# Linear attention in a one-layer encoder kernel: block exponentials with a bias column instead of differences, the root's square on ScalarE, the norm weight in the gate rows, and two filler banks with four for small products

## The chip, the cores and the metric

The kernel runs on one core of a Trainium2 chip. The metric is the device time of one execution in microseconds (us). The kernel before took 1954.07 us (median of three runs, 1953.86 to 1955.78).

## The reference

One layer for 1056 frames at once: a prompt of 1024 and a sample of 32 that goes on from a cached state. All is float32. What concerns this case:

```python
h = rms_norm(x, g_pre_mix)
qa, ka, va, ra, alr, qb, kb, vb, ga, gb = split_cols(h @ w_in)
# branch A, 4 heads, key width 128, value width 256
log_a = log_sigmoid(alr @ w_a2 + b_a2) / 16
b = cumsum(log_a)                      # inside a block
scores[i, j] = sum_c q[i,c] k[j,c] exp(b[i,c] - b[j,c])   for j <= i
o = scores @ v + (q * exp(b)) @ S
S = exp(b_last) * S + (k * exp(b_last - b)).T @ v
o = o * rsqrt(mean(o * o) + eps) * g_gla * silu(ra)       # norm over a head's 256 values
# branch B: 8 heads of softmax attention on a band of 9 chunks of 64 frames
mix = (sigmoid(ga) * (o @ w_br_a) + sigmoid(gb) * (ob @ w_br_b)) @ w_out
x = x + rms_norm(mix, g_post_mix)
# then the convolutional feed-forward part and the per-layer embedding
```

## The kernel before

All frames lie along the free axis (T = 1056 columns), features on the 128 partitions. A product with a weight is three float32r passes (high part by high, low by high, high by low), in three column chunks of 352.

By the clock of the profile the stages are: the first products (to 66 us); the projections that are multiplied in the two-level scheme of `in_strassen` (66 to 322), which store rows of silu(r) and the gates to DRAM; band attention (322 to 590); linear attention (590 to 930); its products with `w_br_a` (to 1052); then the out product, the feed-forward part and the embedding, which the change does not touch.

In both attentions the remaining projections are cut into *filler* units: 24 matmuls into one PSUM bank, given out in thirds by `piece()` between the small products of attention, so that TensorE has work while VectorE (DVE) and ScalarE (ACT) prepare the next ones. `flush()` issues the emptying of the units that are finished (L710 and L728 on ACT, L786 on DVE). The order of PE, DVE and ACT in linear attention is written out by hand (`tc.manual_schedule`): each engine works in the order of the code.

PSUM has eight banks. `PS_BAND = (3, 3, 1)` gives three to fillers (`mm`), three to small products (`one`: turns, sums, outputs, states, decay products) and one double bank to scores (`two`). A tile takes the bank of the tile of its kind that lies as many tiles back as there are banks, and its first writer waits until that one has been read.

Linear attention works through 16 segments `u`, four to a head: 256 frames each, the last one 288 with the sample. Inside a block of 128 frames the decay between two frames is split over levels l = 1 to 6, blocks of 2, 4, ... 64 frames: a difference of `b` to its value at the block's middle (`differences`, L1173), its exponential for the lower and the upper half (`exponentials`, L1191, L1192) and the factor q or k (`factors`, L1205). Level 7 is the distance to the block's end (L1177, L1179, then L1186) and, beside it, exp(b) itself (L1187), with one wide factor (L1199). `key_turns` (L1239) transposes level 7's k for the state; `level_products` (L1217 to L1232) makes the scores; `outputs` the values; `squares_a`, `sums_a`, `roots` and `results` the norm (L1324 to L1359). `results` squares the root once on DVE (L1354), improves it by one Newton step (L1355, L1356), multiplies by the norm weight, a column per row of 128 values (L1358, twice), and by the silu row (L1359). `decays` computes `b` of the next head (L1050 to L1072) in steps between the segments.

The last linear attention segment runs beside the first products with `w_br_b`, whose rows `branch_split` (L1415, L1416) splits.

Of the kernel before, what the change touches and what calls it, by code (L numbers as in the profile page):

```python
# [17 lines left out]
P = 128  # L18
# [31 lines left out]
XFIRST = 0  # L50
PLE_DVE = (1,)
B_BUFS = 1
PS_BAND = (3, 3, 1)
BAND_GATES = (1, 1, 1, 0)
GLA_GATES = (0, 0, 1, 3)
GA_DENSE = 4
# [57 lines left out]
def emit(tc, a):  # L114
# [77 lines left out]
    def col(i):  # L192
        return vec[:, i : i + 1]
# [393 lines left out]
    repsum((0, 0, 4))  # L587
    dq = pool("dq")

    def in_strassen(n1, n2, f, d1, d2):  # L590
        raw = early.pop("raw", None)
        if not raw:
            raw = [tl(wp, [P, KT, P], tag="raw", bufs=2), tl(dp, [P, KT, P], tag="raw2", bufs=2)]
            for r, n in zip(raw, (n1, n2)):
                dma.dma_start(r, a["w_in"][n])
        a11, a12, a21, a22 = raw[0][:, up1], raw[0][:, up2], raw[1][:, up1], raw[1][:, up2]

        def plus(x, y, o):
            t = tl(dq, [P, HK, P], tag="ws", bufs=3)
            with tc.high_priority():  # L600
                ve.tensor_tensor(t, x, y, op=o)
            return t

        def weight(x):
            h = tl(wp, [P, HK, P], F32R, tag="whi", bufs=4)
            l = tl(wp, [P, HK, P], F32R, tag="wlo", bufs=4)
            with tc.high_priority():
                ac.activation(h, x, AF.Copy)
                ve.tensor_tensor(l, x, h, op=ALU.subtract)
            return h, l  # L610
# [12 lines left out]
        c11, c12, c21, c22 = v2(z1[:, one]), v2(z1[:, two]), v2(z2[:, one]), v2(z2[:, two])  # L623
        p1 = v2(tl(dq, [P, HT], tag="p1", bufs=1))
        q = v2(tl(dq, [P, HT], tag="c22", bufs=1))
        X = ps_pair()
        X_ = X[:, :, :HC]
        mul(X, early.pop("a11", None) or weight(a11), "b11", True, True)
        ac.activation(p1, X_, AF.Copy)
        lead = early.pop("a12", None)  # L630
        if lead:
            mul(X, lead, "b21", False, True)
            ac.activation(c11, X_, AF.Copy)
        s1 = plus(a21, a22, ALU.add)
        s2 = plus(s1, a11, ALU.subtract)
        Y = ps_pair()
        Y_ = Y[:, :, :HC]
        mul(Y, weight(s2), "t2", True, True)
        ve.tensor_tensor(c12, p1, Y_, op=ALU.add)
        Z = ps_pair()  # L640
        Z_ = Z[:, :, :HC]
        mul(Z, weight(s1), "t1", True, True)
        ve.tensor_tensor(q, p1, Z_, op=ALU.add)
        if not lead:
            mul(X, weight(a12), "b21", False, True)
            ac.activation(c11, X_, AF.Copy)
        s3 = plus(a11, a21, ALU.subtract)
        mul(Y, weight(s3), "t3", False, True)
        ve.tensor_tensor(c22, q, Y_, op=ALU.add)
        s4 = plus(a12, s2, ALU.subtract)  # L650
        mul(Z, weight(s4), "b22", False, True)
        ve.tensor_tensor(c12, c12, Z_, op=ALU.add)
        ac.activation(z1, z1, f)
        dma.dma_start(d1, z1)
        mul(Y, weight(a22), "t4", False, True)
        ve.tensor_tensor(c21, p1, Y_, op=ALU.add)
        ac.activation(z2, z2, f)
        dma.dma_start(d2, z2)

    for n in range(0, 8, 2):  # L660
        in_strassen(R0 + n, R0 + n + 1, AF.Silu, d_sr[n], d_sr[n + 1])
    for w0, d, top in ((GB0, d_gb, 8), (GA0, d_ga, GA_DENSE)):
        for n in range(0, top, 2):
            in_strassen(w0 + n, w0 + n + 1, AF.Sigmoid, d[n], d[n + 1])
# [374 lines left out]
    def decays(h):  # L1039
# [23 lines left out]
        e = g["e"] = tl(gp, [P, 9], tag="be", bufs=2)  # L1063
        ac.activation(e[:, 0:8], b[:, 0:NP].rearrange("p (n s) -> p n s", s=P)[:, :, P - 1], AF.Exp, scale=-1.0 / TAU)
        ac.activation(e[:, 8:9], b[:, T - 1 : T], AF.Exp, scale=-1.0 / TAU)
        yield
        bo, qo = blocks(b, 1), tl(gp, [P, T // 2], tag="qo", bufs=1)
        g["qo"] = qo
# [93 lines left out]
    def differences(u, ls):  # L1162
        g, h, s, t0, nt = seg(u)
        b = g["b"]
        if ls[0] == 1:
            X[u] = tl(gp, [P, 8, 288], tag="x", bufs=2)
        x = X[u]
        for l in ls:
            if l == 7:
                break  # L1170
            m, w = 1 << l, level_width(l, nt)
            bv = blocks(b[:, t0 : t0 + w], m)
            ve.tensor_tensor(blocks(x[:, l - 1, :w], m), bv, bv[:, :, m - 1 : m].to_broadcast([P, w // (2 * m), 2 * m]), op=ALU.subtract)  # L1173
        if ls[-1] < 7:
            return
        bv = b[:, t0 : t0 + 256].rearrange("p (n s) -> p n s", s=P)
        ve.tensor_tensor(x[:, 6, :256].rearrange("p (n s) -> p n s", s=P), bv[:, :, P - 1 : P].to_broadcast([P, 2, P]), bv, op=ALU.subtract)  # L1177
        if nt > 256:
            ve.tensor_tensor(x[:, 6, 256:nt], b[:, T - 1 : T].to_broadcast([P, NS]), b[:, NP:T], op=ALU.subtract)  # L1179

    def exponentials(u, ls):
        g, h, s, t0, nt = seg(u)
        x = X[u]
        for l in ls:
            if l == 7:
                ac.activation(x[:, 6, :nt], x[:, 6, :nt], AF.Exp, scale=-1.0 / TAU)  # L1186
                ac.activation(x[:, 7, :nt], g["b"][:, t0 : t0 + nt], AF.Exp, scale=-1.0 / TAU)  # L1187
                continue
            m, w = 1 << l, level_width(l, nt)
            xv = blocks(x[:, l - 1, :w], m)  # L1190
            ac.activation(xv[:, :, 0:m], xv[:, :, 0:m], AF.Exp, scale=1.0 / TAU)  # L1191
            ac.activation(xv[:, :, m:], xv[:, :, m:], AF.Exp, scale=-1.0 / TAU)  # L1192
# [148 lines left out]
    def roots(u):  # L1341
        r = R[u]
        n = r["m"].shape[-1]
        y = r["z"] = r["sq"][:, 0, :n]
        ac.activation(y, r["m"], AF.Ln)
        ac.activation(y, y, AF.Exp, scale=-0.5)

    def results(u):
        g, h, s, t0, nt = seg(u)
        r = R.pop(u)  # L1350
        X.pop(u)
        y, ps, ot = r["z"], r["m"], r["ot"]
        t = r["sq"][:, 1, :nt]
        ve.tensor_tensor(t, y, y, op=ALU.mult)  # L1354
        ve.scalar_tensor_tensor(t, t, -0.5, ps, op0=ALU.mult, op1=ALU.mult)  # L1355
        ve.scalar_tensor_tensor(t, t, 1.5, y, op0=ALU.add, op1=ALU.mult)  # L1356
        for j in range(2):
            ve.scalar_tensor_tensor(ot[:, j, :nt], ot[:, j, :nt], col(G_GLA + 2 * h + j), t, op0=ALU.mult, op1=ALU.mult)  # L1358
        ve.tensor_tensor(ot[:, :, :nt], ot[:, :, :nt], r["sr"][:, :, :nt], op=ALU.mult)  # L1359
        dma.dma_start(d_oa[rows(h, t0, nt)].rearrange("j p t -> p j t"), ot[:, :, :nt])  # L1360

# [17 lines left out]
    dma.dma_start(HA[0]["kq"], d_kq.rearrange("j p t -> p j t"))  # L1379
    chain = steps  # L1380
    next(chain)
    differences(0, range(1, 8))
    exponentials(0, range(1, 8))
    piece()
    piece()
    flush()
# [1 line left out]
        turn_values(0, n)  # L1388
    for f in chain:
        pass  # L1390
    factors(0, range(1, 8))
    piece()
    piece()
    turn_values(0, 6)
    turn_values(0, 8)
    while fill["at"] < 3 * 15:
        piece()
    flush()

    def branch_rows():  # L1400
        both = tl(gp, [P, 2, T], tag="kq", bufs=2)
# [23 lines left out]
    for u in range(16):  # L1425
# [26 lines left out]

        level_products(u, (turns, states, piece))
        if u < 15:
            exponentials(u + 1, range(1, 5))
        if u == 15:
            flush()
        score_copies(u, range(-1, 7))
# [1 line left out]
            branch_split(1)  # L1460
        flush()
        if u < 15:
            differences(u + 1, range(5, 8))
            factors(u + 1, range(1, 5))
            exponentials(u + 1, range(5, 8))
        steps_of(piece, 3)
        flush()
        if s < 2 and h:
# [1 line left out]
        outputs(u)  # L1470
        squares_a(u)
        if u < 15:
            factors(u + 1, range(5, 8))
        if u >= 12:
            next(rows_times, None)
        flush()
# [7 lines left out]
        if u == 14:  # L1484
            while fill["at"] < 3 * FIRST:
                piece()
            flush()
            xp.release()
            bo = pool("bo", side="right")
            for x in "hl":  # L1490
                OB[x] = tl(bo, [P, 4, T], F32R, tag="b" + x)
            branch_split(0)
            split_tile()
            gate_rows(1)
# [4 lines left out]
        if u == 13:  # L1499
            next(rows_times, None)  # L1500
            gate_rows(0)
        if u == 15:
            branch_split(2)
    flush()
    piece()
    flush()
# [4 lines left out]
    order.__exit__(None, None, None)  # L1511


    gp.release()
    gc.release()
    op = pool("op")
# [25 lines left out]
    branch_b(3)  # L1542
    rows_split(range(3, 8))
    bo.release()

    psum.release()
    psum = tc.alloc_tile_pool(name="psum_wide", bufs=1, space=bass.MemoryType.PSUM, reuse_waits="tile")
    banks[:] = [MODE, 8 - MODE, 0]

    mp = pool("mp", side="right")  # L1550
    mh = tl(mp, [P, KT, T], F32R, tag="mh")
# [1130 lines left out]
```

## Time and profile before

| | |
|---|---|
| three runs | 1954.07, 1955.78, 1953.86 us |
| the profiled execution | 1952.56 us, of which the span from the first to the last instruction is 1950.6 |
| mean granted TensorE clock | 0.996 |
| busy share of the span | PE 97%, PEld 95%, DVE 66%, ACT 48%, POOL 11% |
| band attention, 322 to 590 us | PE 255.75 of 268 us, DVE 155.89, ACT 161.69 |
| linear attention, 600 to 930 us | PE 323.32 of 330 us, DVE 248.83, ACT 156.39 |

PE is TensorE's matmuls, PEld its weight loads, which overlap with them. A group's line reads: line of the kernel, engine, operation, output from inputs, count, busy time, mean duration in ns, and the idle time ahead of it with what ended that. A line of the waits view reads: the engine, the tile it would write and its line, what it waited for, the total, the number of times, the longest.

### The profile page before, as it was taken

Reading aid. Unit: us, or ns where it says so; the run is one execution under the profiler, and the core shown is the slowest. Engines: PE = TensorE matmul, PEld = TensorE weight load, DVE = VectorE, ACT = ScalarE, POOL = GpSimd, SP = SyncE. Lnnn points to the kernel's source line nnn. Section 1 sums busy time; section 2 is a strip of 40 time slices with the busy share of each in tenths; the row PEclk is TensorE's granted clock in tenths of the full one; section 3 lists DMA queues with packets and bytes.
Section 4 is the critical chain, followed back from the end, with each engine's and each line's share of the span. In section 5 each row is a group of like instructions: output and inputs, shape, how many; then the busy total and the mean of one; then the engine's idle time right before and its main releaser. Section 6 shows DMA issues by size and latency. Waiting matters only on the chain.

```text
span 1950.6 us, 34919 instructions
## 1 busy us (share of the span) xinstructions
PE 1898.7 (97%) x13960; PEld 1861.5 (95%) x13960; DVE 1284.8 (66%) x2367; ACT 931.5 (48%) x1820; POOL 208.0 (11%) x352
## 2 busy tenths in 40 slices
PE   8999999999999999999999999999999999999996
PEld 8999999989999999999999999999999999999996
DVE  6855444555656776777544686877777766558776
ACT  7444345556665455453333455433334345555555
POOL 0000000000001101001220121111111211000112
PEclk9999999999999999999999999999999999999998
DMA  7233335232315546567844246544354559897756
GB/s 279 85 100 111 99 104 156 82 89 81 91 47 154 145 120 160 161 182 216 303 133 127 90 162 205 185 138 138 113 125 111 125 146 304 266 297 240 239 158 106
DMA packets 111119, 300.91 MB, mean 154 GB/s; under 512 B 12452, under 2 KB 34796, under 8 KB 110316
## 3 DMA queue, kind: packets, MB, share of 16 engines
q1 hardware_dynamic: 81500, 205.95, 33.5%
q0 software_dynamic: 28016, 88.05, 16.7%
q10 hardware_dynamic: 1440, 4.69, 0.6%
q8 instruction: 109, 1.79, 0.4%
q14 instruction: 54, 0.44, 0.1%
HBM read 201.20 MB, written 114.09 MB: 162 GB/s over the span
## 4 chain that ended last, share of the span: by engine, by line
PE 76%; DVE 12%; ACT 7%; issue 2%; DMA 2%; ACTq 0%; SPq 0%; DVEq 0%
PE two L1911 6%; PE two L1913 6%; PE two L1912 6%; PE mm L230 5%; PE mm L232 5%; PE mm L231 5%; PE mm L804 4%; PE mm L805 4%; PE mm L806 4%; PE two L2358 4%; PE two L2357 4%; PE two L618 4%; PE two L619 3%; PE two L2356 3%; PE two L620 3%
## 5 line engine op out<-in xcount | busy, mean ns | idle before, releaser
L804 PE MATMUL mm<-xh,whi 128*128 128x352 f32 x696 | 236.6, 340 | 0.0
L806 PE MATMUL mm<-xh,wlo 128*128 128x352 f32 x696 | 225.3, 324 | 0.0
L805 PE MATMUL mm<-xl,whi 128*128 128x352 f32 x696 | 224.6, 323 | 0.0
L2357 PE MATMUL two<-d,whi 128*128 128x264 f32 x616 | 174.8, 284 | 2.7 <-DVE d L2051 2.7
L2358 PE MATMUL two<-d,wlo 128*128 128x264 f32 x616 | 175.5, 285 | 1.2 <-DVE wlo L2100 1.2
L2356 PE MATMUL two<-d,whi 128*128 128x264 f32 x616 | 174.7, 284 | 0.1
L1913 PE MATMUL two<-mh,wlo 128*128 128x264 f32 x576 | 163.0, 284 | 0.0
L1912 PE MATMUL two<-ml,whi 128*128 128x264 f32 x576 | 162.9, 284 | 0.0
L1911 PE MATMUL two<-mh,whi 128*128 128x264 f32 x576 | 161.2, 284 | 0.0
L804 PEld LDWEIGHTS mm<-xh,whi 128*128 128x128 f32 x696 | 131.3, 189 | 1.7
L805 PEld LDWEIGHTS mm<-xl,whi 128*128 128x128 f32 x696 | 131.2, 189 | 0.4
L806 PEld LDWEIGHTS mm<-xh,wlo 128*128 128x128 f32 x696 | 130.5, 188 | 0.0
L2357 PEld LDWEIGHTS two<-d,whi 128*128 128x128 f32 x616 | 115.8, 188 | 3.3 <-DVE d L2051 3.3
L2358 PEld LDWEIGHTS two<-d,wlo 128*128 128x128 f32 x616 | 115.6, 188 | 1.7 <-DVE wlo L2100 1.7
L2356 PEld LDWEIGHTS two<-d,whi 128*128 128x128 f32 x616 | 116.4, 189 | 0.3 <-ACT d L2050 0.3
L1913 PEld LDWEIGHTS two<-mh,wlo 128*128 128x128 f32 x576 | 108.4, 188 | 0.0
L1912 PEld LDWEIGHTS two<-ml,whi 128*128 128x128 f32 x576 | 108.4, 188 | 0.0
L1911 PEld LDWEIGHTS two<-mh,whi 128*128 128x128 f32 x576 | 107.3, 188 | 0.0
L940 ACT ACTIVATE s<-s,sm 128x640 f32<-128x640 f32 (+5 forms) x72 | 50.6, 703 | 97.1 <-DVE sm L939 97.0
L1901 ACT ACTIVATE whi<-ws 128x512 fp32r<-128x512 f32 x72 | 45.2, 631 | 97.9 <-PE two L1912 72.7
L618 PE MATMUL two<-th,whi 128*128 128x264 f32 x320 | 90.8, 284 | 0.0
L619 PE MATMUL two<-tl,whi 128*128 128x264 f32 x320 | 90.8, 284 | 0.0
(610 smaller groups left out, 5996.9 us busy)
## 6 DMA issues: line engine op xcount, KB each, us to landing
raw<-in_w_in SPq DMA_DIRECT2D x52, 512.0 KB, 3.7
uraw<-d_b SPq DMA_DIRECT2D x34, 528.0 KB, 4.6
d_b<-av POOLq DMA_DIRECT2D x33, 528.0 KB, 4.0
d_ws<-in_w_down POOLq DMA_DIRECT2D x24, 704.0 KB, 6.5
raw<-in_w_up SPq DMA_DIRECT2D x27, 512.0 KB, 3.6
wraw<-d_ws SPq DMA_DIRECT2D x16, 704.0 KB, 6.4
d_b<-gc POOLq DMA_DIRECT2D x11, 792.0 KB, 4.9
sraw<-in_w_up SPq DMA_DIRECT2D x17, 512.0 KB, 4.7
```

What stands on the lines that cost most here:

```text
L230: pe.matmul(ps, h, xh(kt), start=(first and i == 0), stop=False)
L618: pe.matmul(ps[:, j, :HC], w[0][:, k], x[0](k, s), start=st, stop=False, skip_group_check=True)
L619: pe.matmul(ps[:, j, :HC], w[0][:, k], x[1](k, s), start=False, stop=False, skip_group_check=True)
L804: pe.matmul(ps, wh, h[:, k, s], start=(k == 0), stop=False)
L805: pe.matmul(ps, wh, l[:, k, s], start=False, stop=False)
L806: pe.matmul(ps, wl, h[:, k, s], start=False, stop=(k == cnt - 1))
L1911: pe.matmul(ps[:, j, :HC], w[0][:, k], x[0][:, k, s], start=st, stop=False, skip_group_check=True)
L1912: pe.matmul(ps[:, j, :HC], w[0][:, k], x[1][:, k, s], start=False, stop=False, skip_group_check=True)
L1913: pe.matmul(ps[:, j, :HC], w[1][:, k], x[0][:, k, s], start=False, stop=sp_, skip_group_check=True)
L2356: pe.matmul(o, wh, xh_[:, s], start=(k == 0 and p in (0, 4, 5)), stop=False, skip_group_check=True)
L2357: pe.matmul(o, wh, xl_[:, s], start=False, stop=False, skip_group_check=True)
L2358: pe.matmul(o, wl, xh_[:, s], start=False, stop=(k == HD - 1 and p in (3, 4, 6)), skip_group_check=True)
```

## The change

Six edits go together.

1. PSUM in the two attentions: two banks for fillers, four for small products. A `flush` now follows each piece in two loops that run fillers to a mark. The pool for the last products, (4, 4, 0), is opened before `branch_b(2)` instead of after `rows_split`.
2. The norm weight goes into the eight silu rows: one more ACT copy with a scale column, 128x1056, for each row in `in_strassen`. `results` multiplies both halves of a head by the root in one instruction with a broadcast.
3. `decays` leaves columns of `b` at the ends and middles of the blocks of 128, scaled (`refs`, four small ACT instructions per head).
4. Levels 6 and 7 have no difference any more. ACT takes the exponential of `b` itself with a column of `refs` as its bias: four instructions of 64 columns for level 6, two of 128 (a third of 32 in the last segment of a head) for level 7.
5. These exponentials come ahead of the first emptying in a segment; level 7's factor and those of levels 1 to 4 and 6 come ahead of level 5's exponential. In the first segment level 7's factor comes first.
6. The root is squared on ACT, behind the root itself. `branch_split(2)` of the last segment stands behind `squares_a` instead of behind `roots`.

```diff
-PS_BAND = (3, 3, 1)
+PS_BAND = (2, 4, 1)
...
-    def in_strassen(n1, n2, f, d1, d2):
+    def in_strassen(n1, n2, f, d1, d2, gain=None):
...
         ac.activation(z1, z1, f)
+        if gain is not None:
+            ac.activation(z1, z1, AF.Copy, scale=col(gain))
         dma.dma_start(d1, z1)
...
         ac.activation(z2, z2, f)
+        if gain is not None:
+            ac.activation(z2, z2, AF.Copy, scale=col(gain + 1))
         dma.dma_start(d2, z2)
...
-        in_strassen(R0 + n, R0 + n + 1, AF.Silu, d_sr[n], d_sr[n + 1])
+        in_strassen(R0 + n, R0 + n + 1, AF.Silu, d_sr[n], d_sr[n + 1], G_GLA + n)
...
+        refs = g["refs"] = tl(gp, [P, 25], tag="refs", bufs=2)
+        ends = b[:, 0:NP].rearrange("p (n s) -> p n s", s=P)
+        ac.activation(refs[:, 0:8], ends[:, :, P - 1], AF.Copy, scale=-1.0 / TAU)
+        ac.activation(refs[:, 8:9], b[:, T - 1 : T], AF.Copy, scale=-1.0 / TAU)
+        ac.activation(refs[:, 9:17], ends[:, :, P // 2 - 1], AF.Copy, scale=-1.0 / TAU)
+        ac.activation(refs[:, 17:25], ends[:, :, P // 2 - 1], AF.Copy, scale=1.0 / TAU)
...
         for l in ls:
-            if l == 7:
-                break
             m, w = 1 << l, level_width(l, nt)
...
-        bv = b[:, t0 : t0 + 256].rearrange("p (n s) -> p n s", s=P)
-        ve.tensor_tensor(x[:, 6, :256].rearrange("p (n s) -> p n s", s=P), bv[:, :, P - 1 : P].to_broadcast([P, 2, P]), bv, op=ALU.subtract)
-        if nt > 256:
-            ve.tensor_tensor(x[:, 6, 256:nt], b[:, T - 1 : T].to_broadcast([P, NS]), b[:, NP:T], op=ALU.subtract)
...
             if l == 7:
-                ac.activation(x[:, 6, :nt], x[:, 6, :nt], AF.Exp, scale=-1.0 / TAU)
+                for o in range(0, nt, P):
+                    n, w = (t0 + o) // P, min(P, nt - o)
+                    ac.activation(x[:, 6, o : o + w], g["b"][:, t0 + o : t0 + o + w], AF.Exp, scale=1.0 / TAU, bias=g["refs"][:, n : n + 1])
                 ac.activation(x[:, 7, :nt], g["b"][:, t0 : t0 + nt], AF.Exp, scale=-1.0 / TAU)
+                continue
+            if l == 6:
+                for o in range(0, 256, 64):
+                    up_, n = o // 64 % 2, (t0 + o) // P
+                    ac.activation(x[:, 5, o : o + 64], g["b"][:, t0 + o : t0 + o + 64], AF.Exp, scale=(-1.0 if up_ else 1.0) / TAU,
+                                  bias=g["refs"][:, 9 + 8 * up_ + n : 10 + 8 * up_ + n])
                 continue
...
+        ac.activation(r["sq"][:, 1, :n], y, AF.Square)
...
-        ve.tensor_tensor(t, y, y, op=ALU.mult)
...
-        for j in range(2):
-            ve.scalar_tensor_tensor(ot[:, j, :nt], ot[:, j, :nt], col(G_GLA + 2 * h + j), t, op0=ALU.mult, op1=ALU.mult)
+        ve.tensor_tensor(ot[:, :, :nt], ot[:, :, :nt], t.unsqueeze(1).to_broadcast([P, 2, nt]), op=ALU.mult)
...
-            exponentials(u + 1, range(1, 5))
+            exponentials(u + 1, (1, 2, 3, 4, 6, 7))
...
-            differences(u + 1, range(5, 8))
-            factors(u + 1, range(1, 5))
-            exponentials(u + 1, range(5, 8))
+            differences(u + 1, (5,))
+            factors(u + 1, (7, 1, 2, 3, 4, 6))
+            exponentials(u + 1, (5,))
...
-            factors(u + 1, range(5, 8))
+            factors(u + 1, (5,))
+        else:
+            branch_split(2)
...
+    repsum((MODE, 8 - MODE, 0))
     gp.release()
```

TensorE's instructions keep their order throughout, and so do GpSimd's. Three places show what moves on the other two engines. First ACT in the second segment of the last head, from the last small exponentials to the second emptying of a filler unit (`mm` into `ev`); `x` holds the levels, `b` the sums. Before:

```order
L1191 ACTIVATE x_9322<-x_9322 128x8x16
L1192 ACTIVATE x_9322<-x_9322 128x8x16
L710 ACTIVATE ev_9308<-mm_9342 128x352
L1191 ACTIVATE x_9322<-x_9322 128x4x32
L1192 ACTIVATE x_9322<-x_9322 128x4x32
L1191 ACTIVATE x_9322<-x_9322 128x2x64
L1192 ACTIVATE x_9322<-x_9322 128x2x64
L1186 ACTIVATE x_9322<-x_9322 128x256
L1187 ACTIVATE x_9322<-b_8641 128x256
L710 ACTIVATE ev_9308<-mm_9424 128x352
```

And in the changed kernel, whose line numbers differ by 4 to 10 (L714 is the emptying):

```order
L1201 ACTIVATE x_9351<-x_9351 128x8x16
L1202 ACTIVATE x_9351<-x_9351 128x8x16
L1196 ACTIVATE x_9351<-b_8666,refs_9084 128x64 x4
L1190 ACTIVATE x_9351<-b_8666,refs_9084 128x128 x2
L1191 ACTIVATE x_9351<-b_8666 128x256
L714 ACTIVATE ev_9339<-mm_9371 128x352
L1201 ACTIVATE x_9351<-x_9351 128x4x32
L1202 ACTIVATE x_9351<-x_9351 128x4x32
L714 ACTIVATE ev_9339<-mm_9456 128x352
```

Seven instructions have come ahead of the first emptying, and four have left the way to the second.

Next DVE in the same segment, from the score copies to the second half of the norm (`kq` holds k and q). Before:

```order
L1258 COPY_PREDICATED scores_1112_6723<-masks_3238,two_9328 128x2x64
L1173 TENSOR_TENSOR x_9322<-b_8641 128x256 x2
L1177 TENSOR_TENSOR x_9322<-b_8641 128x256
L1205 TENSOR_TENSOR x_9322<-x_9322,kq_8476 128x256 x4
L1330 SCALAR_TENSOR_TENSOR sq_1475_9465<-sq_1475_9465 128x256
L1333 TENSOR_TENSOR y_1477_9469<-sq_1475_9465,y_1476_9468 128x256
L1205 TENSOR_TENSOR x_9322<-x_9322,kq_8476 128x256 x2
L1199 TENSOR_TENSOR x_9322<-x_9322,kq_8476 128x2x256
```

And now:

```order
L1268 COPY_PREDICATED scores_1112_6731<-masks_3246,two_9357 128x2x64
L1181 TENSOR_TENSOR x_9351<-b_8666 128x256
L1209 TENSOR_TENSOR x_9351<-x_9351,kq_8502 128x2x256
L1215 TENSOR_TENSOR x_9351<-x_9351,kq_8502 128x256 x5
L1340 SCALAR_TENSOR_TENSOR sq_1479_9497<-sq_1479_9497 128x256
L1343 TENSOR_TENSOR y_1481_9501<-sq_1479_9497,y_1480_9500 128x256
L1215 TENSOR_TENSOR x_9351<-x_9351,kq_8502 128x256
```

Two differences are gone, and level 7's wide factor, on which the next segment's turns depend, stands first instead of last.

Last DVE ahead of the first segment (`ev` holds the first head's `b` there, `qo` the odd frames' factors). Before:

```order
L1173 TENSOR_TENSOR x_6736<-ev_6295 128x256 x6
L1177 TENSOR_TENSOR x_6736<-ev_6295 128x256
L1069 TENSOR_TENSOR qo_6792<-ev_6295 128x528
L1072 TENSOR_TENSOR qo_6792<-qo_6792,kq_6730 128x528
L1205 TENSOR_TENSOR x_6736<-x_6736,kq_6730 128x256 x6
L1199 TENSOR_TENSOR x_6736<-x_6736,kq_6730 128x2x256
```

And now:

```order
L1181 TENSOR_TENSOR x_6749<-ev_6303 128x256 x5
L1079 TENSOR_TENSOR qo_6806<-ev_6303 128x528
L1082 TENSOR_TENSOR qo_6806<-qo_6806,kq_6738 128x528
L1209 TENSOR_TENSOR x_6749<-x_6749,kq_6738 128x2x256
L1215 TENSOR_TENSOR x_6749<-x_6749,kq_6738 128x256 x6
```

The wide factor has come ahead of the six others.

More of the change, by code (lines that the diff above doesn't have):

```diff
@@ L1173, in differences @@
             ve.tensor_tensor(blocks(x[:, l - 1, :w], m), bv, bv[:, :, m - 1 : m].to_broadcast([P, w // (2 * m), 2 * m]), op=ALU.subtract)
-        if ls[-1] < 7:
-            return
-        bv = b[:, t0 : t0 + 256].rearrange("p (n s) -> p n s", s=P)
-        ve.tensor_tensor(x[:, 6, :256].rearrange("p (n s) -> p n s", s=P), bv[:, :, P - 1 : P].to_broadcast([P, 2, P]), bv, op=ALU.subtract)
-        if nt > 256:
-            ve.tensor_tensor(x[:, 6, 256:nt], b[:, T - 1 : T].to_broadcast([P, NS]), b[:, NP:T], op=ALU.subtract)
     def exponentials(u, ls):
@@ L1381, in emit @@
     next(chain)
-    differences(0, range(1, 8))
-    exponentials(0, range(1, 8))
+    differences(0, range(1, 6))
+    exponentials(0, (7, 6, 1, 2, 3, 4, 5))
     piece()
@@ L1390, in emit @@
         pass
-    factors(0, range(1, 8))
+    factors(0, (7, 1, 2, 3, 4, 5, 6))
     piece()
@@ L1397, in emit @@
         piece()
-    flush()
+        flush()
     def branch_rows():
@@ L1486, in emit @@
                 piece()
-            flush()
+                flush()
             xp.release()
@@ L1501, in emit @@
             gate_rows(0)
-        if u == 15:
-            branch_split(2)
     flush()
@@ L1544, in emit @@
     bo.release()
-    psum.release()
-    psum = tc.alloc_tile_pool(name="psum_wide", bufs=1, space=bass.MemoryType.PSUM, reuse_waits="tile")
-    banks[:] = [MODE, 8 - MODE, 0]
     mp = pool("mp", side="right")
```

## The prediction

> **What bounds the kernel now.** I read the page first: busy times, then the chain that ended last.
>
> ```profile
> PE 1898.7 (97%) x13960; PEld 1861.5 (95%) x13960; DVE 1284.8 (66%) x2367; ACT 931.5 (48%) x1820; POOL 208.0 (11%) x352
> PE 76%; DVE 12%; ACT 7%; issue 2%; DMA 2%; ACTq 0%; SPq 0%; DVEq 0%
> ```
>
> TensorE is busy 97% of the span and its own work is 76% of the chain. DVE's 66% and ACT's 48% cost only where TensorE stands still for them. The change touches no matmul, so all it can win is TensorE's idle time, and all it can lose is new idle time. The next view is the busy time by stage: the projections whose rows get the gain, then the linear attention (its start, and two halves).
>
> ```profile
> 66.00:322.00 256.00, 254.22 (x2024) 253.02 (x2023) 136.70 (x202) 105.99 (x161) 8.27 (x32) 1.00 0.37 119
> 590.00:600.00 10.00, 7.99 (x60) 7.82 (x59) 4.80 (x13) 6.22 (x20) 0.52 (x1) 1.00 0.65 229
> 600.00:760.00 160.00, 157.17 (x1075) 150.57 (x1074) 119.60 (x309) 78.45 (x230) 17.70 (x28) 1.00 0.52 134
> 760.00:930.00 170.00, 166.15 (x1116) 158.06 (x1115) 129.23 (x314) 77.94 (x222) 19.19 (x25) 1.00 0.65 189
> ```
>
> After the window's length the columns are PE, PEld, DVE, ACT, POOL, granted clock, DMA share and GB/s. In the linear attention TensorE idles 2.01 + 2.83 + 3.85 = 8.7 us of 340; from 600 on DVE is busy 75%, ACT 47%; the granted clock is 1.00 throughout. What TensorE waited for stands in the waits view, first for 590 to 940, then the three largest of the whole run, which lie in the band attention (322 to 590).
>
> ```profile
> PE one L1239 <- DVE x L1199: 2.0, 1, 2.0
> PE one L1050 <- ACT b L1052: 1.8, 2, 1.1
> PE mm L804 <- DVE ev L786: 0.8, 1, 0.8
> PE one L1338 <- ACT y L1332: 0.7, 2, 0.4
> PE one L1239 <- ACT vt L1152: 0.7, 1, 0.7
> PE one L1239 <- DVE sq L1355: 0.7, 1, 0.7
> PE mm L805 <- DVE bl L1416: 0.5, 1, 0.5
> PE one L1151 <- ACT ev L710: 0.4, 1, 0.4
> ...
> PE two L933 <- DVE sm L939: 4.9, 8, 1.3
> PE one L987 <- DVE pt L949: 3.5, 9, 0.5
> PE one L911 <- DVE vs L908: 3.1, 3, 1.0
> ```
>
> Columns: total, times, longest. The first eight are 7.6 of the 8.7 us. They are of two kinds. L1239 behind L1199 waits for data. L1050 behind L1052, and L1239 behind L1152 or L1355, do not read what those write: they wait until a small-product bank (`one`) has been emptied. L911 behind L908 is the same in the band.
>
> **The change part by part.** The durations, all of one instruction, in linear attention (DVE first, then ACT):
>
> ```profile
> L1173 DVE TENSOR_TENSOR x<-b 128x256 f32<-128x256 f32 x60 | 21.8, 417 | 0.0
> L1358 DVE SCALAR_TENSOR_TENSOR ot<-ot,vec,sq 128x256 f32<-128x256 f32 x24 | 10.6, 482 | 0.4
> L1359 DVE TENSOR_TENSOR ot<-ot,sr 128x512 f32<-128x512 f32 x12 | 8.3, 691 | 0.4
> L1354 DVE TENSOR_TENSOR sq<-sq 128x256 f32<-128x256 f32 x12 | 5.0, 418 | 5.9 <-ACT sq L1346 5.8
> L1177 DVE TENSOR_TENSOR x<-b 128x256 f32<-128x256 f32 x12 | 5.0, 416 | 0.0
> ...
> L1191 ACT ACTIVATE x<-x 128x128 f32<-128x128 f32 x78 | 23.6, 302 | 90.0 <-DVE x L1173 90.0
> L710 ACT ACTIVATE ev<-mm 128x352 f32<-128x352 f32 x26 | 11.6, 446 | 4.1 <-PE mm L806 4.1
> L1346 ACT ACTIVATE sq<-sq 128x256 f32<-128x256 f32 x12 | 5.0, 417 | 0.4
> L1051 ACT ACTIVATE ev<-one,vec 128x352 f32<-128x352 f32 x9 | 5.0, 556 | 0.0
> L1186 ACT ACTIVATE x<-x 128x256 f32<-128x256 f32 x12 | 4.8, 401 | 0.0
> ```
>
> DVE, per segment: two differences go (0.417 + 0.416), the root's square goes (0.418), two gain products become one wide one (2 x 0.482 - 0.691 = 0.273). Together 1.52 us, over 16 segments 24 us of DVE time. TensorE sees only what of this ended one of its waits.
>
> ACT, per segment: L1191, its partner of the same size and L1186 (0.302 + about 0.30 + 0.401 = 1.00) become four exponentials of 64 columns and two of 128, each with a bias column; the square is added at 0.417. No row shows a 64-wide exponential. Below, it costs 0.25 (the 128-wide 0.302 less half the columns at (0.401 - 0.302)/128, 0.05); above, 0.36 if the column adds what L1051 shows over L710 of the same shape (0.11). So 4 x 0.25 to 0.36, plus 2 x 0.30 to 0.41, plus 0.417, less 1.00: 1.0 to 1.7 us more, 16 to 27 us over the stage, on an engine that idles half of it. I take 1.4, the middle. The four small rows per head add about 0.2 us each to head preparation, beside waiting time. The Trainium skill (ScalarE: Activation LUTs, What ACT_TABLE_LOAD costs) gives 186 ns plus 0.833 ns per element and 93 ns for each pointer operand; by that a biased 64-wide exponential would take 332 ns, an estimate near my upper bound, and the sum would not move; the trace's 0.11 for the column agrees.
>
> Data waits. At the start of linear attention (DVE's timeline, then TensorE's):
>
> ```profile
> 596.70 2.10 DVE L1205 TENSOR_TENSOR x<-x,kq 128x256 f32<-128x256 f32 x6
> 598.71 0.68 DVE L1199 TENSOR_TENSOR x<-x,kq 128x512 f32<-128x512 f32 x1
> 599.54 0.41 PE L1239 MATMUL one<-ident,x 128*128 128x128 f32 x2 [2.01 <-DVE x L1199]
> ```
>
> L1199 gets ahead of the six L1205 and two differences leave the queue in front: it ends 2 us or more earlier, before TensorE arrives at 597.5. Gain 2.0. The same reordering inside the segments removes short waits of this kind; what the eight rows leave of the 8.7 us is 1.1, and I give 0.8 of that to it and to the shorter DVE queue. L1338 loses 0.4 of its 0.7, where DVE comes earlier to its partner.
>
> Bank waits, linear attention: a fourth `one` bank removes 1.8 + 0.7 + 0.7 = 3.2. The Trainium skill (Perfetto Trace Analysis, Identifying Performance Opportunities) says that gaps which repeat on the engine that should be full can mean too few buffers in PSUM. These rows agree for `one`; the same rule speaks against taking a bank from the fillers, which follows below.
>
> Each of these dozen waits also breaks the overlap of successive matmuls: in the rows below a filler matmul is 0.32 long and the next starts 0.16 later, so a stop costs 0.16 beside its idle time. That adds 1.9. Sum in linear attention: 2.0 + 0.8 + 0.4 + 3.2 + 1.9 = 8.3.
>
> Band. The fourth bank removes L911's 3.1, but see what follows (TensorE, then DVE):
>
> ```profile
> 369.31 0.23 PE L911 MATMUL one<-ident,ev 64*32 64x64 f32 x1 [1.02 <-DVE vs L908]
> 372.59 1.52 PE L987 MATMUL one<-pt,vs 128*128 128x256 f32 x12
> ...
> 369.17 0.81 DVE L939 CUSTOM_DVE_ANT_0 s<-two,bias 128x640 f32<-128x640 f32 x1
> 371.53 1.02 DVE L949 TENSOR_TENSOR pt<-one,pt 128x512 fp32r<-128x512 f32 x2 [1.53 <-ACT pt L948]
> ```
>
> L987 needs what L949 writes, and L949 ends at 372.55; TensorE got there at 372.59 without slack. A microsecond won at 369 is waited again at 372. I take 0.5 of the three, with 0 and 3.1 + 3 x 0.16 = 3.6 as ends.
>
> Two filler banks. A unit now waits for the emptying of the unit two before, not three. In linear attention the emptying often queues behind the exponentials on ACT. The tightest place and a typical tight one (ACT, then TensorE's first matmul of the unit after next):
>
> ```profile
> 643.03 0.45 ACT L728 ACTIVATE kq<-mm 128x352 f32<-128x352 f32 x1
> 644.16 0.32 PE L804 MATMUL mm<-xh,whi 128*128 128x352 f32 x1
> 644.32 0.32 PE L805 MATMUL mm<-xl,whi 128*128 128x352 f32 x1
> ...
> 863.31 0.45 ACT L710 ACTIVATE ev<-mm 128x352 f32<-128x352 f32 x1
> 865.58 0.33 PE L804 MATMUL mm<-xh,whi 128*128 128x352 f32 x1
> ```
>
> Between emptied and needed lie 0.68 and 1.82 us. The six biased exponentials and L1187 now stand ahead of these emptyings: 4 x 0.2 + 2 x 0.2 + 0.31 at back-to-back pitch, about 1.5, up to 2.0 with the column's price. The first place then waits about 1.0, places like the second 0 to 0.2; the second emptying in a segment comes earlier by the same. I take 1.2 for the stage. L1357, the square, stands ahead of an emptying that L1151 waits for: 0.35 more there. At the end (905 to 930) the units are short and DVE empties them behind L1416; with a split moved ahead I take 0.3.
>
> Hidden at nothing: eight gain copies in the projections, as long as this row,
>
> ```profile
> L653 ACT ACTIVATE ev<-ev 128x1056 f32<-128x1056 f32 x10 | 10.9, 1089 | 2.3 <-DVE ev L652 2.3
> ```
>
> 8.7 us of ACT time. ACT is busy 106 of 256 us there and writes weight parts microseconds ahead of their use; uncovered, each copy would cost up to 1.09. The loads that move on SP serve later stages, where the window 590 to 930 has DMA at 0.5 to 0.65; I cost them at nothing, and up to 1 us if a late row stalls the products at 951. The four filler banks for the last products stay at nothing too.
>
> Sum: -8.3 - 0.5 + 1.2 + 0.35 + 0.3 = -7.0. The profiled execution took 1952.56 us (1950.6 of span and 2.0 around it), 1.5 below the median of the three runs, 1954.07. So 1945.6 for one like it, **1947.0** on the median.
>
> **The rivals.**
> - *Half is waited again.* As in the band, TensorE arrives earlier at the next product that needs DVE or ACT. For it: DVE is at 75% in this stage. Against it: DVE itself loses 24 us there. -3 or so: 1951, within what a measurement of this kernel can tell from no change (0.2%, 3.9 us).
> - *Slower: fillers queue behind the exponentials.* If the seven instructions take 4 us rather than 1.5 to 2, the filler banks run dry in the eight segments of fifteen where less than 4 us lie between emptied and needed. The two above would wait 3.3 and 2.2; with the looser ones I estimate 13 over the eight. Against gains of 8.3 + 0.5 it ends at +4 or so: 1958. It decides from a delay of about 3.3 us. Against it: 0.11 per column and 0.2 pitch give 2. For it: no row shows a 64-wide exponential with a bias column.
> - *The band's banks pay in full.* L933 and L987 do not grow and the whole 3.6 comes: -10, with the filler cost at nothing -12: 1942.
> - *Nothing reaches TensorE.* The bank waits only change their releaser: 1954.
>
> **How the numbers follow.** Forecast (1944 to 1950) 0.55, half waited again 0.16, slower by the fillers (with late rows at 951) 0.15, band in full 0.09, nothing 0.05. Faster by over 0.2% are the forecast, the band and a little of the halves: 0.67. Within 0.2%: 0.19. Slower: 0.14. The range runs from 1941.5 (band in full) to 1955 (half and nothing), leaving out most of the slower case and a thin tail below.
>
> **What the changed profile would show.** Right: no L1239 wait of 2 us near 597; no wait of decay products (L1050's) or of L1239 for a bank; L911's wait gone and those of L933 and L987 grown by nearly as much; one or two new waits of `mm` for an emptying on ACT, under 1.5 us in all; DVE busy about 24 us less and ACT some 30 more over the run. Wrong: `mm` waits behind ACT in many segments, biased exponentials well over 0.36 us, or a new wait of the last products for attention rows.

## The result, and the profile after

The changed kernel took 1946.21 us (median of five, 1945.59 to 1946.51) against 1954.07 (median of five of before, 1952.49 to 1957.41): a ratio of 0.9959, 95% interval 0.9948 to 0.9969. 1947.0 was forecast. The profiled executions took 1952.56 us before and 1946.21 after, spans 1950.6 and 1944.1.

The busy times of the changed kernel, then its windows (the columns as before):

```profile
PE 1897.5 (98%) x13960; PEld 1861.9 (96%) x13960; DVE 1261.7 (65%) x2299; ACT 966.4 (50%) x1912; POOL 209.6 (11%) x352
```

```profile
66.00:322.00 256.00, 254.23 (x2023) 253.00 (x2022) 136.73 (x201) 115.16 (x169) 8.26 (x32) 1.00 0.37 119
590.00:600.00 10.00, 9.93 (x71) 9.50 (x70) 4.54 (x12) 7.59 (x27) 1.04 (x2) 1.00 0.56 201
600.00:760.00 160.00, 159.24 (x1097) 153.51 (x1096) 111.33 (x281) 92.93 (x284) 17.19 (x28) 1.00 0.55 142
760.00:930.00 170.00, 166.31 (x1121) 159.34 (x1120) 119.34 (x279) 87.05 (x242) 22.57 (x26) 1.00 0.67 201
```

In linear attention TensorE idles 0.07 + 0.76 + 3.69 = 4.5 us, where it was 8.7. DVE is 23 us less busy over the run, ACT 35 more. What TensorE still waits for between 590 and 940, and in the band:

```profile
PE mm L808 <- DVE ev L790: 1.4, 2, 0.8
PE one L1161 <- ACT ev L714: 0.9, 1, 0.9
PE mm L808 <- ACT kq L732: 0.8, 2, 0.5
PE mm L230 <- DVE gb L790: 0.7, 1, 0.7
PE mm L808 <- ACT ev L714: 0.2, 1, 0.2
...
PE two L937 <- DVE sm L943: 7.5, 11, 1.3
PE one L991 <- DVE pt L953: 3.5, 9, 0.4
```

The data wait near 597 and all the waits for a small bank are gone; all that are left in linear attention are waits for an emptying of a filler bank, or of the unit that a turn reads (L1161). In the band the sum of the largest waits went from 11.5 to 11.0.

The new operations, from the groups by form (the first four in linear attention, the last in the projections):

```profile
L1196 ACT ACTIVATE x<-b,refs 128x64 f32<-128x64 f32 x48 | 12.7, 336 | 0.0
L1190 ACT ACTIVATE x<-b,refs 128x128 f32<-128x128 f32 x24 | 8.2, 389 | 0.0
L1357 ACT ACTIVATE sq<-sq 128x256 f32<-128x256 f32 x12 | 5.0, 419 | 0.4
L1367 DVE TENSOR_TENSOR ot<-ot,sq 128x512 f32<-128x512 f32 x12 | 8.3, 692 | 0.4
...
L655 ACT ACTIVATE ev<-ev,vec 128x1056 f32<-128x1056 f32 x4 | 4.7, 1182 | 0.1
```

### The profile page after: what moved, and what is told of

Same layout as the page of the kernel before. It is cut to its first block, busy times and chain, and to the rows that moved or that the text cites. A ratio compares the mean times of both kernels' runs of the same rounds, so it can differ in the third digit from the quotient of the medians.

```text
span 1944.1 us, 34934 instructions
## 1 busy us (share of the span) xinstructions
PE 1897.5 (98%) x13960; PEld 1861.9 (96%) x13960; DVE 1261.7 (65%) x2299; ACT 966.4 (50%) x1912; POOL 209.6 (11%) x352
## 4 chain that ended last, share of the span: by engine, by line
PE 78%; DVE 11%; ACT 7%; DMA 2%; issue 2%; POOL 0%; ACTq 0%; SPq 0%; DVEq 0%; POOLq 0%
PE two L1917 6%; PE two L1918 6%; PE two L1919 6%; PE mm L230 5%; PE mm L232 5%; PE mm L231 5%; PE mm L808 4%; PE mm L810 4%; PE mm L809 4%; PE two L2363 4%; PE two L2364 4%; PE two L2362 4%; PE two L618 4%; PE two L619 4%; PE two L620 3%; PE two L1242 2%
## 5 line engine op out<-in xcount | busy, mean ns | idle before, releaser
L808 PE MATMUL mm<-xh,whi 128*128 128x352 f32 x696 | 236.6, 340 | 1.0 <-ACT kq L732 0.8
L808 PEld LDWEIGHTS mm<-xh,whi 128*128 128x128 f32 x696 | 131.3, 189 | 3.2 <-ACT kq L732 1.2
```

The lines of the kernel that those rows point to most:

```text
L808: pe.matmul(ps, wh, h[:, k, s], start=(k == 0), stop=False)
```

## The experiments

Times are medians, with the lowest and highest, in five rounds; the kernel before had 1954.0 to 1954.3 beside them (1951.1 to 1956.8). Runs are named by what they are: first parts of the change put into the kernel before, then parts taken out of the changed kernel, and some that go beyond it. TensorE's instructions keep their order in all of them, so the same matmul can be looked up in two traces; where a run gains or loses "on the same matmuls", that is the difference of their starts, with the places given in the times of before.

**The banks alone** (in the kernel before)

```diff
-PS_BAND = (3, 3, 1)
+PS_BAND = (2, 4, 1)
# and a flush() after each piece in the two loops; the last pool opened before branch_b(2)
```

> The kernel before with the banks alone: two for fillers, four for small products, a flush after each piece in the two loops, the last pool opened earlier. Theory (my terms): the three kinds of bank waits in linear attention go, 3.2 us of idle and about 0.9 of broken overlap, and 0.5 in the band; with the old order nothing but four small exponentials pairs stands ahead of the first emptying, so two filler banks cost nothing there, but 2 to 3 us between 905 and 925, where the split still stands late. Net -1 to -2 us; the 2.0 us wait near 597 stays. Rival (the bank waits only change their releaser): L1050's and L1239's waits stay in other names, 0 or slower by the 2 to 3 us.

1954.18 us (1951.56 to 1961.39), ratio 1.0001 (0.9991 to 1.0011): nothing. Its waits, and a window behind the first of them:

```profile
PE mm L804 <- DVE ev L786: 2.7, 1, 2.7
PE one L1239 <- DVE x L1199: 1.8, 1, 1.8
PE mm L230 <- DVE gb L786: 1.6, 1, 1.6
```

```profile
912.00:916.00 4.00, 3.36 (x11) 3.36 (x12) 3.86 (x9) 0.73 (x1) 0.00 (x0) 0.50 0.78 267
```

The bank waits went, as the theory had it, not to other names. On the same matmuls this run gains 4.6 us between 600 and 912. The end took it back, 6.5 us between 912 and 945: 2.7 and 1.6 us of waits for emptyings, and with the long one the granted clock fell to 0.50 for 6.8 us (912.0 to 918.8). That last part no theory had.

**The order alone** (in the kernel before: levels 6 and 7 still by differences)

```diff
-    factors(0, range(1, 8))
+    factors(0, (7, 1, 2, 3, 4, 5, 6))
...
-            differences(u + 1, range(1, 5))
+            differences(u + 1, (1, 2, 3, 4, 6, 7))
...
-            exponentials(u + 1, range(1, 5))
+            exponentials(u + 1, (1, 2, 3, 4, 6, 7))
...
-            factors(u + 1, range(1, 5))
+            factors(u + 1, (7, 1, 2, 3, 4, 6))
```

> The kernel before with the order alone: the differences and exponentials of levels 6 and 7 ahead of the first emptying, level 7's factor first, also at the start; no bias column, three filler banks. Theory: the 2.0 us wait near 597 goes, and about 1 us of the short ones behind level 7's factor; nothing is paid, since three filler banks bear the delay. -2.5 to -3.5 us, bank waits stay. Rival (the order helps only with the lighter DVE): two more differences stand ahead of the score copies, and half or more of the gain is waited again: 0 to -1.5.

1949.31 us (1948.79 to 1950.04), ratio 0.9976 (0.9967 to 0.9986): 4.9 us by the medians, more than the theory's 2.5 to 3.5, though the interval (2.7 to 6.4 us) reaches into it. The rival, at most 1.5, falls.

**The bias columns alone, at the old places** (in the kernel before)

```diff
-                ac.activation(x[:, 6, :nt], x[:, 6, :nt], AF.Exp, scale=-1.0 / TAU)
+                for o in range(0, nt, P):
+                    ...  # as in the change, and level 6 likewise
...
-            differences(u + 1, range(5, 8))
+            differences(u + 1, (5,))
```

> The kernel before with the bias columns alone: levels 6 and 7 without a difference, at the old places in the order, and the columns in decays; three filler banks. Theory: DVE 13 us less busy, ACT 12 to 16 more; TensorE sees 0.8 of the 2.0 us near 597 and a few tenths: -0.5 to -1.5 us. Rival (DVE's load bounds the stage, so any work taken off it pays): -4 or more. Rival (biased pieces of 64 columns cost TensorE): slower.

1965.1 us (1963.04 to 1965.46), ratio 1.0054 (1.0041 to 1.0066): 11 us slower. Only the third line of the expectation had the sign, and not the cause. Its largest wait was 0.7 us in before (L1338 there); then ACT's and TensorE's timelines in a segment, and the same TensorE row of before:

```profile
PE one L1344 <- ACT y L1338: 4.9, 6, 1.4
```

```profile
650.39 1.05 ACT L1192 ACTIVATE x<-ev,refs 128x64 f32<-128x64 f32 x4
651.34 0.89 ACT L1186 ACTIVATE x<-ev,refs 128x128 f32<-128x128 f32 x3
653.34 0.58 ACT L1330 ACTIVATE ot<-one 128x512 f32<-128x512 f32 x1
```

```profile
655.54 0.39 PE L1344 MATMUL one<-y,onesHr 128*128 128x256 f32 x1 [1.38 <-ACT y L1338]
```

```profile
651.86 0.38 PE L1338 MATMUL one<-y,onesHr 128*128 128x256 f32 x1 [0.39 <-ACT y L1332]
```

At the old place the exponentials of levels 6 and 7 stand straight ahead of the output's copy and squares (L1330 to L1338), and TensorE waits for their end already in before. What ACT gets more there, TensorE waits longer: from the first exponential behind DVE's last difference to the output's copy ACT takes 3.37 us (649.97 to 653.34), in before 2.34 (647.31 to 649.65), and TensorE's 0.39 became 1.38. The work that DVE lost ended no wait. Listed waits are not all of the 11 us: in the profiled execution the granted clock in linear attention was also 0.50 twice for 3.4 us, from 600.0 and from 903.7.

**Bias columns and order, three filler banks** (in the kernel before)

The two edits above together.

> The kernel before with the bias columns and the new order, three filler banks, the rest as before. Theory: the 11 us of the bias columns at the old place are the square sums' wait for ACT, behind exponentials that stood ahead of them; ahead of the first emptying the same exponentials fill time in which ACT waited for DVE, so the 11 us vanish: 1948.5 to 1950, like the order alone. Rival (64-column pieces with a bias cost by themselves): 1955 or more. Rival (bias and order together beat the order by the lighter DVE): 1947.5 or less.

1947.87 us (1946.33 to 1948.7), ratio 0.9966 (0.9954 to 0.9979). The 11 us have vanished, as the theory said, 0.6 below its range; the third line's 1947.5 was missed by 0.4. But the ranges of this run and of the order alone do not meet: 1.4 us lie between the medians, and 1.4 between the same matmuls at 1000. So with three filler banks the bias columns, once in the new order, did pay a little. In that order the exponentials stand ahead of the first emptying, where ACT had time:

```profile
640.43 1.05 ACT L1192 ACTIVATE x<-ev,refs 128x64 f32<-128x64 f32 x4
646.84 0.60 ACT L1330 ACTIVATE ot<-one 128x512 f32<-128x512 f32 x1 [0.76 <-PE one L1304]
```

ACT now waits 0.76 us for the output before it copies it; it no longer comes late, and the wait behind L1338 is gone from the list.

**The norm weight and the square alone** (in the kernel before: edits 2 and the square of 6)

> The kernel before with the norm weight in the silu rows and the square on ACT alone; three filler banks, old order. Theory: eight copies of 1.1 to 1.2 us beside the projections cost nothing, the window 66 to 322 keeps its length within 0.3 us; the square puts 0.35 ahead of one emptying, and the bank wait behind L1355 shortens by the square: -0.5 to +0.5 us. Rival (the copies are uncovered): up to +8.7 us in the window 66 to 322. Rival (DVE's load bounds the stage): -2 or more.

1953.41 us (1951.47 to 1955.01), ratio 0.9997 (0.9988 to 1.0006): no difference. TensorE is busy 254.22 of the 256 us from 66 on, as before. The wait behind L1355 did not shorten (0.7 us still); the one for the emptying that the square stands ahead of rose from 0.4 to 0.8.

**Three and three banks in the changed kernel**

```diff
-PS_BAND = (2, 4, 1)
+PS_BAND = (3, 3, 1)
```

> The changed kernel with three banks for fillers and three for small products again. Theory: the bank waits of the decay products and of L1249 come back, 2 to 3 us with the broken overlap, against 1.0 us of mm waits behind ACT that go and about 1 at the end; slower by 1 to 2.5 us than the changed kernel. Rival (the fourth small bank is only waited again): no slower. Rival (the two filler banks cost more than the fourth pays): faster by 1 or more.

1946.95 us (1945.35 to 1948.15), 0.7 above the changed kernel's median with overlapping ranges. By the time the first rival holds best: the bank edit is worth nothing that can be told. Its waits, its last window, and the same window of the changed kernel:

```profile
PE one L1054 <- ACT b L1056: 2.3, 2, 1.4
PE one L1161 <- ACT ev L714: 0.8, 1, 0.8
PE one L1249 <- ACT vt L1162: 0.7, 1, 0.7
PE one L1249 <- DVE sq L1365: 0.7, 1, 0.7
```

```profile
890.00:940.00 50.00, 50.00 (x318) 48.51 (x317) 32.45 (x64) 17.50 (x33) 10.09 (x8) 1.00 0.79 270
```

```profile
890.00:940.00 50.00, 47.87 (x297) 45.74 (x296) 29.80 (x59) 15.54 (x24) 12.20 (x8) 1.00 0.76 256
```

3.7 us of waits for small banks return, and 2.1 at the end and 1.0 behind ACT go. With three filler banks TensorE never stops from 890 to 940. Two matmuls, one in the last segment and one behind it, in this run and then in the changed kernel:

```profile
906.77 0.32 PE L809 MATMUL mm<-bl,whi 128*128 128x352 f32 x1
938.60 0.33 PE L230 MATMUL mm<-bh,whi 128*128 128x352 f32 x1
```

```profile
903.19 0.32 PE L809 MATMUL mm<-bl,whi 128*128 128x352 f32 x1
937.89 0.33 PE L230 MATMUL mm<-bh,whi 128*128 128x352 f32 x1
```

At the end of the band the changed kernel is 0.54 us ahead (L1037 at 587.02 against 587.56), at the first pair 3.58, at the second 0.71. So the bank edit wins 3.0 us in linear attention and pays 2.9 at its end. The rival has the time right and not the reason: the fourth bank's gain is not waited again, it is paid back by the fillers.

**The third split late again** (in the changed kernel: `branch_split(2)` behind `roots`)

> The changed kernel with the third split of the last segment back behind roots, as before. Theory: with two filler banks the unit near 907 waits for an emptying that then stands behind four more split halves on DVE: +1.5 to +2.5 us. Rival (the move is beside the path): within 0.5 us.

1949.63 us (1946.61 to 1951.89): 3.4 us slower, more than expected. One wait of 3.2 us took the place of two of 1.4 together, and the granted clock was 0.50 behind it for 3.4 us (910.9 to 914.3).

**The biased exponentials twice** (in the changed kernel, each issued a second time into the same place)

> The changed kernel with each biased exponential issued twice: about 2 us more on ACT ahead of the first emptying of each segment, nothing else. It prices the slower rival: with two filler banks the free time left between emptied and needed in the changed kernel is 0.05, 0.4, 0.4, 1.0, 1.3, 1.5, 1.7, 1.8 and 1.8 us in nine segments, so 2.1 us more would make 9 us of waits by that sum, 6 to 9 after what each wait gives the next. Rival (ACT is half idle, so it takes this in its stride): under 2 us.

1964.01 us (1962.44 to 1970.49): 18 us slower than the changed kernel, twice what was expected. ACT's timeline in the longest segment, of the changed kernel and of this one, and this one's waits:

```profile
639.16 1.06 ACT L1196 ACTIVATE x<-ev,refs 128x64 f32<-128x64 f32 x4
640.12 0.90 ACT L1190 ACTIVATE x<-ev,refs 128x128 f32<-128x128 f32 x3
641.26 0.45 ACT L732 ACTIVATE kq<-mm 128x352 f32<-128x352 f32 x1
```

```profile
647.37 2.58 ACT L1198 ACTIVATE x<-ev,refs 128x64 f32<-128x64 f32 x8
649.85 2.11 ACT L1191 ACTIVATE x<-ev,refs 128x128 f32<-128x128 f32 x6
652.21 0.44 ACT L732 ACTIVATE kq<-mm 128x352 f32<-128x352 f32 x1
```

```profile
PE mm L808 <- ACT kq L732: 8.2, 5, 3.0
PE mm L808 <- ACT ev L714: 4.5, 6, 1.6
```

The block ahead of the emptying grew from 2.10 to 4.84 us there, more than the 2.1 us that doubling was to add, and `mm` waits behind ACT grew from 1.0 to 12.7. The granted clock was 0.50 for 3.4 us behind two of them (from 653 and from 820). This is the slower rival at work. The profiled execution, 1970.49, is the longest of the five, but 5.7 us of its excess lie ahead of linear attention; from the end of the band to 945 it loses 18.4 us to the changed kernel on the same matmuls, as the medians have it.

**The square late** (in the changed kernel)

```diff
-        ac.activation(r["sq"][:, 1, :n], y, AF.Square)     # in roots
...
+        ac.activation(t, y, AF.Square)                      # in results
```

> The changed kernel with the square, still on ACT, issued in results, behind the emptying that it stood ahead of. Theory: the waits near 656, 774 and 831 (0.3, 0.6 and 1.0 us), whose emptying follows the square, lose up to 0.35 each: -0.8 to -1.1 us. Rival (they are set by other work ahead on ACT): 0. Rival (results comes too late and its bank is waited for): slower by 0.5 or more.

1944.89 us (1943.75 to 1946.95), 1.3 below the changed kernel. The interval of this run's ratio, 0.9943 to 0.9968, holds the changed kernel's, so the time alone does not decide. The waits do: L1161 went from 0.9 to 0.4 and L808 behind ACT from 1.0 to 0.4.

```profile
PE mm L808 <- ACT kq L732: 0.4, 2, 0.3
PE one L1161 <- ACT ev L714: 0.4, 1, 0.4
```

**Differences instead of bias columns** (in the changed kernel: edits 3 and 4 undone, all else kept)

> The changed kernel with levels 6 and 7 from differences on DVE again, in the changed order and with the changed banks. Theory: in this order the bias columns take DVE work that did not end a wait, and put 0.8 us more on ACT ahead of the first emptying; without them the mm waits behind ACT shrink: within 1 us of the changed kernel, either way. Rival (the lighter DVE is what pays): 2 us slower or more. Rival (the bias columns still cost, as they did at the old place): 3 us faster or more.

1945.21 us (1943.81 to 1946.29), ratio 0.9953 (0.9941 to 0.9966): 1.0 below the changed kernel, within its expectation. In this order and with two filler banks the bias columns, the change's largest edit, pay nothing. Why they gained with three and not with two is not shown.

**The late square, and three and three banks in the last segment** (in the changed kernel)

```diff
         if u:
             results(u - 1)
+        if u == 15:
+            repsum((3, 3, 1))
```

> The changed kernel with the square in results (as in the run with the late square) and the banks set back to three for fillers and three for small products from the last segment on. Theory: the waits between 905 and 925 for emptyings on DVE (0.9 + 0.7 + 0.7 us and their broken overlap) go, as they were absent with three filler banks throughout; the middle keeps what four small banks give. About 2.5 us faster than the late square alone: 1942 to 1943. Rival (the products after the segment only wait later for the attention rows): no faster than 1944.5.

1949.11 us (1947.68 to 1950.02): slower than the late square alone by 4.2. The waits at the end went, but the switch made its own (TensorE, ACT, and a window behind):

```profile
887.95 1.47 PE L1227 MATMUL one<-kq 128*128 128x128 f32 x6 [3.75 <-ACT ev L714]
```

```profile
887.46 0.45 ACT L714 ACTIVATE ev<-mm 128x352 f32<-128x352 f32 x1
```

```profile
889.00:891.00 2.00, 2.00 (x11) 1.67 (x11) 1.50 (x3) 0.00 (x0) 0.00 (x0) 0.50 0.66 219
```

The first small product in the new pool waits for the last emptying of the old one, 3.75 us, and the granted clock is 0.50 behind it. The rival named another cause.

**Four small banks up to the last segment** (in the kernel before: the banks as in the first run, and the same switch)

> The kernel before with four small banks and two filler banks up to the last segment, and three and three in it. Theory: the banks alone came to nothing because 4 to 5 us won in the segments before were lost at 890 to 940; without that loss 3 to 4 us faster than before: 1950 to 1951. Rival (time won in the middle is lost at the end whatever the banks): 1953 or more.

1956.51 us (1954.48 to 1961.32): slower. The rival's "1953 or more" has the time and not the cause, which is the same wait at the switch (4.8 us). The middle can be read from the trace (of the longest of its eleven runs) all the same: between 620 and 889 the same matmuls gain 4.7 us on before, as the theory had it.

## Why the prediction was right, point by point

The sum was -7.0 between profiled executions; they lie 6.35 apart. Its terms against the traces:

- **The wait near 597** (2.0): gone. L1209, the old L1199, now ends at 596.77, and TensorE comes at 596.92.

```profile
596.09 0.68 DVE L1209 TENSOR_TENSOR x<-x,kq 128x512 f32<-128x512 f32 x1
```

- **Bank waits in linear attention** (3.2): gone, and back when the fourth bank is taken away.
- **The band** (0.5, not 3.6): 11.5 became 11.0. The wait of 1.02 at 369.31 became one of 0.81 a few matmuls on, as the rows of before let expect, if at L937 and not at L991:

```profile
369.76 0.42 PE L937 MATMUL two<-kh,qs 128*128 128x320 f32 x1 [0.81 <-DVE sm L943]
```

- **Two filler banks** (1.2 ahead of the end): `mm` waits behind ACT of 1.0, the largest 0.5 where 1.0 was expected.
- **The square ahead of an emptying** (0.35): L1161's wait rose from 0.4 to 0.9.
- **Biased exponentials** (0.25 to 0.36 for 64 columns, a block of 1.5 to 2.0): 0.336, and a block of 1.86 plus what the third piece of a last segment adds (2.10). The column's price, 0.11 from L1051 and L710, is 0.09 here (0.389 against 0.302). The Trainium skill's 93 ns for a pointer operand (ScalarE: Activation LUTs, What ACT_TABLE_LOAD costs) agrees with that and with the gain copy, 1.182 against 1.089.
- **Broken overlap** (1.9): between 588 and 945 the changed kernel gains 6.2 us on the same matmuls, of which 4.2 is idle time; 2.0 is left. That is a remainder and not a count: seven waits are still listed there, where ten were.
- **The gain copies** (0): TensorE busy 254.23 of 256 us, 254.22 before.

The term that was mis-sized is the end, "I take 0.3". Between 912 and 945 the changed kernel loses 1.7 us on before (8.94 ahead became 7.20). That is a balance: with three filler banks the same order gains 1.1 there, so two filler banks cost 2.9, and with them the late split would cost 3.4 more. Up to there the bank edit won about what the sum gave it: 3.0 us in linear attention (3.2 of waits and 1 of overlap, less 1.2) and 0.65 in the band (0.5). In all it was worth 0.7 by the medians, where my sum had about 3. Order, bias, weight and split without it gave 7.3 by their medians, and 6.0 on the same matmuls of linear attention, where I had some 4: 1.5 near 597, 1.1 at the end, and 3.4 inside the segments, where my terms for short waits, L1338 and their overlap, less the square's 0.35, come to under 2. So each mechanism was at work, but the total came out since the two errors are of one size, and that is luck.

Order alone gave 4.9 by the medians but 2.5 between the profiled executions (1952.56 and 1950.03). Its trace shows where the rest went: at 1000 it is 4.1 us ahead of before on the same matmuls, and it loses 1.4 of that between 1600 and 1700, in a stage that the change does not touch, where its granted clock is 0.50 for 6.8 us (from 1612) and that of before's profiled execution is not. Other executions of before seem to pay for such stretches, too: of its 58 runs beside the experiments the eight with a mean granted clock of 0.994 took 1955.5 us on average, the fifteen with 0.997 took 1952.7. That the wait near 597 is what halves the clock in some of them is argued: two of the runs that kept it show it, the profiled execution of before does not.

Of the rivals, the slower one was the nearest. A block of about 4.8 instead of 2.1 us cost 18 us. The waits behind ACT grew by 11.7, near the 13 that I had estimated; the halved clock and the overlap, which I had left out of that rival, come on top. By a straight line between the two runs, (18 - 8) us slower and 8 us faster than before, the break-even lies at about 3.3, where I had put it; that line is an estimate. "Half is waited again" held in the band, where most was, and not in linear attention.

## What to carry to other kernels

Ask which engine's instruction ends the wait at that place, not which engine is busier: taking 11.5 us of busy time off DVE (1284.8 to 1273.3) cost 11 us while its replacement stood ahead of a step that TensorE waited for, and nothing where ACT had been idle. A buffer moved from one kind of tile to another is priced at both ends, and where the units are shortest above all: here it won 3.0 us and paid 2.9. When two traces keep an engine's order, compare the starts of the same instruction: that shows where an edit wins and where it loses, which the total hides. An order that brings a late operand forward may be worth more than the work that it was changed together with.

## What the runs showed of the hardware that was not expected

A long wait of TensorE can cost more than its length. With waits of 2.7 and 3.75 us the granted clock stood at 0.50 for 6.8 us, with one of 3.2 us for 3.4, with one of 4.8 us for 13.7. At 2.0 us it went both ways: the same wait near 599.6, in the kernel before and in the one with the bias columns alone, with the window behind it in each:

```profile
600.00:602.00 2.00, 2.00 (x17) 2.00 (x15) 1.34 (x4) 1.98 (x9) 0.55 (x1) 1.00 0.34 42
```

```profile
600.00:602.00 2.00, 2.00 (x9) 2.00 (x8) 1.43 (x4) 1.92 (x9) 0.48 (x1) 0.50 0.37 42
```

17 matmuls against 9 in the same 2 us. In the second the clock was back at 1.00 after 3.4 us, and the same matmul, 0.09 us later than in before at 599.7, was 1.66 later at 607. The length of the wait is not the whole rule: at 903.7 in the run with the bias columns alone the clock fell for 3.4 us behind a wait of 0.86 us. The Trainium skill (TensorE: Matmul & The Clock Gate, What's actually happening) lets the clock fall to half after an idle window of about 3.4 us that runs freely; here less idle time was enough, in some executions.

The doubled exponentials write the place that the one ahead of them has just written, and started later: the 64-column ones followed each other after 0.24 us (four to 640.12 from 639.16), the doubled ones after 0.31 (eight to 649.85 from 647.37). One by one in the trace the second onto a place starts 0.36 to 0.37 us after the first, which lasts 0.33 to 0.34, and the next place 0.25 to 0.26 after that: the second write did not overlap the first.
